# Reordering the opening of a two-layer hybrid decoder trunk on one Trainium2 core

## The chip, the cores and the metric

The kernel runs on one core of a Trainium2 chip. The metric is the device time of one execution in microseconds; the number to predict is the median over several runs. Engines are called PE (matrix products), DVE (vector), ACT (scalar), POOL and SP (which here only issues loads).

## What is computed

Each of two layers scales, shifts and projects its input, runs two attentions, and then a feed-forward part; scale and shift come from a condition vector `c`. The change touches only the beginning of the first layer:

```python
mod = jax.nn.silu(c) @ w_ada + b_ada                  # c: 1 x 1024, w_ada: 1024 x 6144
sh1, sc1, gt1, sh2, sc2, gt2 = jnp.split(mod, 6, axis=-1)
h = adaln(rms_norm(x, g_mix), sh1, sc1)               # x: 256 x 1024;  h * (1 + sc1) + sh1
proj = h @ w_in
q_a, k_a, v_a, q_b, k_b, v_b, gate_a, gate_b = jnp.split(proj, IN_OFFSETS, axis=-1)
```

All data is float32. `x` is 256 tokens (two tiles `t` of 128) by 1024 features (eight tiles `k` of 128).

## The kernel before

**Products in three parts.** An operand is split into a rounded high part and the rest, a low part. A product is three PE products: high by high, high by low, low by high. Before, the helper `mm3` (lines 505 to 507) issues the three one after the other. A block of weights of 512 KB ("half": two feature tiles of 512 columns) is loaded as float32 into `wraw`, rounded by ACT into the high part (line 423), and DVE subtracts it to give the low part (lines 429 and 918). `Stream` keeps three raw buffers of two halves and, in this stage, four slots `w0` to `w3` for split halves; a raw buffer takes its next load when both its halves are split, a slot when its products are done.

**The opening** (`lead`) computes `q_b`, `k_b` and `v_b` of the first layer, in four quarters of two feature tiles, since a quarter needs only the shift and scale of its 256 features. A quarter has three halves (one each for `q_b`, `k_b`, `v_b`), so 3 x 2 feature tiles x 2 token tiles x 3 parts = 36 products of 128x512. For its shift and scale a quarter needs `silu(c)` times eight 128x512 blocks of `w_ada`. These come as four "pieces" of two blocks (32 loads of 256 KB over all quarters). DVE sums them: `ada_quarter` (lines 313 and 315), one multiply-add `aq` per block, accumulated elementwise, 128 partitions in parallel. Then PE transposes the sum in four blocks (line 291), and DVE reduces along the row to a column (line 297), adds the bias and multiplies by the gain (lines 301 and 304), giving columns `sh` and `s1`. With those DVE makes `hf` (line 927), ACT the high part `hT_hi` (line 929), and DVE the low part `hT_lo` (line 933).

**Order.** The whole opening stands under a manual schedule: each engine executes in the order in which `lead` writes the code, and a waiting instruction holds all behind it on its engine. Which loads come in which order is written in `LOADS`, how many sum steps and weight splits lie between is in `AHEAD`, `LEAD0`, `READY`, `LEAD`. All loads go through SP's queue. The tables for the rotary embedding are made here too: `rope_sin` on ACT (lines 347 and 348, each with a load of a function table), `rope_tables` on DVE (line 366). After `lead` come `k_a` (128x256 products), `q_a`, the gates, and in between the steps of head norm, rotary embedding (lines 727 to 778) and attention (lines 793 to 857) for the heads.

Of the kernel before, what the change touches and what calls it, by code (L numbers as in the profile page):

```python
# [68 lines left out]
Q3 = 3  # L69
GAINS = 1  # L70
POW_LAG = 2

LOADS = "aaaarw4wawaaa"
AHEAD = (0, 2, 0)
LEAD0 = (0, 1, 0, 1, 5)
READY = (2, 0)
LEAD = (("h", "VhV", "v"), ("vh", "V", "v"), ("hVhV", "", "v"), ("hV", "", "vvvv"))
# [5 lines left out]
def kernel(ctx: ExitStack, tc: tile.TileContext, io):  # L85
# [42 lines left out]
    def load_x():  # L128
        nc.sync.dma_start(c8, io["c"][0].rearrange("(p k) -> p k", k=KT))
        nc.sync.dma_start(pos_i, io["positions"][0].rearrange("(t p) -> p t", p=P))  # L130
        nc.sync.dma_start(invf, io["cpack"][:, 0:HALF])
        for t in range(NT):
            nc.sync.dma_start(x_sb[:, t, :], io["x"][0, t * P:(t + 1) * P, :])
            if t == 0:
                nc.sync.dma_start(ident, io["cpack"][:, HALF:HALF + P])

    def load_rows():
        nc.sync.dma_start(grow[0:4 * KT, :], io["grow"])
        for l in range(DEPTH):
            o = (4 + 6 * l) * KT  # L140
            nc.sync.dma_start(grow[o:o + 6 * KT, :], io["b_ada"][l].rearrange("(r c) -> r c", c=P))
# [19 lines left out]

    def silu_c():
# [3 lines left out]
        nc.vector.tensor_scalar(out=cs, in0=cs, scalar1=0.5, scalar2=None, op0=ALU.mult)  # L166

# [139 lines left out]
    def ada_quarter(u):  # L307

        acc = ring(512, "aq")
        for k in range(KT):  # L310
# [15 lines left out]
    def rope_angles():  # L326
        nc.vector.tensor_copy(pos_f, pos_i)
        ang = work.tile([P, NT, HALF], F32, tag="rt", name="ang", bufs=3)
        for t in range(NT):
            nc.vector.tensor_scalar(out=ang[:, t, :], in0=invf, scalar1=pos_f[:, t:t + 1], scalar2=None, op0=ALU.mult)  # L330
        ns = [work.tile([P, NT, HALF], F32, tag="rt", name=nm("rtn"), bufs=3) for _ in range(2)]
# [532 lines left out]
    def lead():  # L864

        V = nc.vector
        stream.hold = True
        load_x()
        pieces = iter(range(16))

        def load_ada(n):
            for _ in range(n):
                ada_load(next(pieces))

        for o in LOADS:
            if o == "r":
                load_rows()
            elif o == "w":
                stream.load_next()
            elif o.isdigit():  # L880
                stream.between = lambda n=int(o): load_ada(n)
            else:
                load_ada(1)
        silu_c()
        rope_angles()
        stats = [ln_stats(t, (0, 1)) for t in range(NT)]
# [315 lines left out]
```

## Time and profile before

| | us |
|---|---|
| median of 3 runs (763.82 to 766.08) | 765.72 |
| the profiled execution: its time | 763.05 |
| its span, first to last instruction | 761.3 |
| PE busy | 723.2 (95%) |
| DVE busy | 600.1 (79%) |
| ACT busy | 431.3 (57%) |

A busy PE is not PE at its peak, because its instructions overlap and their ends are modelled; for products, the distance from one start to the next tells the cost. PEclk is the clock that was granted to PE, 1.00 being 2.4 GHz and 0.50 being 1.2 GHz.

### The profile page before, as it was taken

How to read it: one execution, taken by the hardware profiler on the slowest of the kernel's cores; microseconds unless marked ns; L12 is line 12 of the kernel's file. 1: busy time of each engine (PE TensorE's matmuls, PEld its weight loads, DVE VectorE, ACT ScalarE, POOL GpSimd, SP SyncE). 2: the span in 40 equal slices, each digit the busy share in tenths (PEclk: the TensorE clock that was granted, in tenths of full speed). 3: DMA queues.
4: the chain of work that ended last, by engine and by line, in shares of the span. 5: the costliest groups of instructions: out<-in, count | busy, mean ns of one | idle time of the engine just before them, and what ended most of it. 6: DMA issues, size and time to landing. Idle time of an engine off the chain costs nothing.

```text
span 761.3 us, 12132 instructions
## 1 busy us (share of the span) xinstructions
PE 723.2 (95%) x4601; PEld 638.2 (84%) x4601; DVE 600.1 (79%) x1107; ACT 431.3 (57%) x817; POOL 30.7 (4%) x23
## 2 busy tenths in 40 slices
PE   3879889999989999999998999999999999999997
PEld 2558678899869899899987888989988998999996
DVE  6978989989999988989889878987879755445532
ACT  6336369874457655554545457676546755555550
POOL 1003110000000000000000311000000000000000
PEclk9999999999999999999999999999999999999999
DMA  8968458867859999998893653663661856565511
GB/s 294 391 234 277 140 164 283 282 218 273 279 165 294 379 348 318 333 321 318 308 306 112 217 170 112 206 211 122 233 240 62 285 190 198 168 204 182 181 42 55
DMA packets 110538, 173.45 MB, mean 228 GB/s; under 512 B 4744, under 2 KB 68488, under 8 KB 110480
## 3 DMA queue, kind: packets, MB, share of 16 engines
q1 hardware_dynamic: 110480, 172.68, 66.8%
q8 instruction: 36, 0.59, 0.3%
q14 instruction: 22, 0.18, 0.1%
HBM read 171.62 MB, written 1.05 MB: 227 GB/s over the span
## 4 chain that ended last, share of the span: by engine, by line
PE 74%; DVE 11%; DMA 8%; ACT 2%; issue 2%; POOL 1%; SPq 0%; DVEq 0%; ACTq 0%; POOLq 0%
PE tmp L510 12%; PE tmp L512 11%; PE tmp L511 11%; PE acc L507 11%; PE acc L505 11%; PE acc L506 11%; DMA araw<-in_w_ada_dram 3%; DVE ada L262 2%; DVE w L429 2%; PE tmp L853 1%; POOL rs L734 1%; PE tmp L837 1%; PE acc L793 1%; DMA wraw<-in_w_out_dram 1%; DMA gt<-in_w_ada_dram 1%
## 5 line engine op out<-in xcount | busy, mean ns | idle before, releaser
L429 DVE TENSOR_TENSOR w<-wraw,w 128x1024 fp32r<-128x1024 f32 x144 | 174.4, 1220 | 51.5 <-ACT w L423 50.3
L423 ACT CAST w<-wraw 128x1024 fp32r<-128x1024 f32 x150 | 155.5, 1048 | 79.7 <-PE acc L507 46.4
L510 PE MATMUL tmp<-hT_hi,w 128*128 128x256 f32 x480 | 140.1, 292 | 1.1 <-DVE alo L857 1.1
L512 PE MATMUL tmp<-hT_hi,w 128*128 128x256 f32 x480 | 135.9, 283 | 0.0
L511 PE MATMUL tmp<-hT_lo,w 128*128 128x256 f32 x480 | 135.7, 283 | 0.0
L262 DVE SCALAR_TENSOR_TENSOR ada<-araw,cs,ada 128x512 f32<-128x512 f32 x140 | 104.3, 745 | 4.1 <-DMA araw<-in_w_ada_dram 2.9
L510 PEld LDWEIGHTS tmp<-hT_hi,w 128*128 128x128 f32 x480 | 91.5, 191 | 8.0 <-issue 4.4
L511 PEld LDWEIGHTS tmp<-hT_lo,w 128*128 128x128 f32 x480 | 91.7, 191 | 0.7
L512 PEld LDWEIGHTS tmp<-hT_hi,w 128*128 128x128 f32 x480 | 91.6, 191 | 0.3 <-issue 0.3
L505 PE MATMUL acc<-w,uhi 128*128 128x512 f32 x192 | 75.4, 393 | 0.0
L506 PE MATMUL acc<-w,uhi 128*128 128x512 f32 x192 | 74.9, 390 | 0.0
L507 PE MATMUL acc<-w,ulo 128*128 128x512 f32 x192 | 74.9, 390 | 0.0
L1093 ACT ACTIVATE relu<-tmp 128x256 f32<-128x256 f32 x56 | 21.5, 384 | 68.9 <-PE tmp L512 68.9
L507 PEld LDWEIGHTS acc<-w,ulo 128*128 128x128 f32 x192 | 36.1, 188 | 7.6
L505 PEld LDWEIGHTS acc<-w,uhi 128*128 128x128 f32 x192 | 36.1, 188 | 6.9
L506 PEld LDWEIGHTS acc<-w,uhi 128*128 128x128 f32 x192 | 36.1, 188 | 6.8
L505 PE MATMUL acc<-w,hT_hi 128*128 128x512 f32 x88 | 36.7, 419 | 2.6 <-ACT hT_hi L929 2.6
L507 PE MATMUL acc<-w,hT_lo 128*128 128x512 f32 x88 | 36.1, 410 | 2.8 <-DVE hT_lo L933 2.8
L506 PE MATMUL acc<-w,hT_hi 128*128 128x512 f32 x88 | 36.2, 411 | 1.2 <-DVE w L429 0.7
L423 ACT CAST kv<-wraw 128x1024 fp32r<-128x1024 f32 x21 | 22.1, 1053 | 24.6 <-PE acc L507 19.8
L429 DVE TENSOR_TENSOR ahi<-wraw,ahi 128x1024 fp32r<-128x1024 f32 x18 | 22.0, 1221 | 15.0 <-ACT ahi L423 14.9
L429 DVE TENSOR_TENSOR kv<-wraw,kv 128x1024 fp32r<-128x1024 f32 x21 | 25.6, 1221 | 9.6 <-ACT kv L423 9.5
(221 smaller groups left out, 1726.2 us busy)
## 6 DMA issues: line engine op xcount, KB each, us to landing
araw<-in_w_ada_dram SPq DMA_DIRECT2D x80, 512.0 KB, 6.6
wraw<-in_w_up_dram SPq DMA_DIRECT2D x32, 1024.0 KB, 5.6
wraw<-in_w_down_dram SPq DMA_DIRECT2D x32, 1024.0 KB, 5.0
wraw<-in_w_in_dram SPq DMA_DIRECT2D x28, 1024.0 KB, 6.1
wraw<-in_w_out_dram SPq DMA_DIRECT2D x8, 1024.0 KB, 4.9
wraw<-in_w_in_dram SPq DMA_DIRECT2D x12, 512.0 KB, 6.6
wraw<-in_w_o_swa_dram SPq DMA_DIRECT2D x8, 512.0 KB, 3.6
wraw<-in_w_o_moba_dram SPq DMA_DIRECT2D x8, 512.0 KB, 5.3
```

The source lines that it names most:

```text
L262: nc.vector.scalar_tensor_tensor(out=acc, in0=raw[:, k, :], scalar=cs[:, kk:kk + 1], in1=(bz if kk == 0 else acc), op0=ALU.mult, op1=ALU.add)
L423: nc.scalar.copy(hi, r)
L429: ins = nc.vector.tensor_tensor(out=lo, in0=r, in1=hi.bitcast(F32), op=ALU.subtract)
L505: nc.tensor.matmul(ps, lhsT=lh, rhs=rh, start=start, stop=False)
L506: nc.tensor.matmul(ps, lhsT=lh, rhs=rl, start=False, stop=False)
L507: nc.tensor.matmul(ps, lhsT=ll, rhs=rh, start=False, stop=stop)
L510: nc.tensor.matmul(ps, lhsT=wh, rhs=ah, start=start, stop=False)
L511: nc.tensor.matmul(ps, lhsT=wh, rhs=al, start=False, stop=False)
L512: nc.tensor.matmul(ps, lhsT=wl, rhs=ah, start=False, stop=stop)
L734: nc.gpsimd.tensor_tensor(out=rs, in0=ss, in1=mhalf[:, :NT * nh].rearrange("p (t h) -> p t h", h=nh), op=ALU.pow)
L793: nc.tensor.matmul(pss[i][:, os], lhsT=qT[hp, pair, qs], rhs=kT[hp, kp, ks], start=True, stop=True)
L1093: nc.scalar.activation(r, ps, AF.Relu)
```

## The change

- The sums of quarters 1 and 2 move from DVE to PE. `pe_sums` multiplies each block by a 128x32 operand `cz` whose first column is `silu(c)` and whose others are zero: eight float32 products of 32x512. The eight write four groups of 32 PSUM partitions, two products to a group. ACT copies the result (`arow`), and four products by a column of ones (`columns`) sum over partitions and turn the row into columns. Quarters 0 and 3 stay on DVE (`dve_sums`), but use `columns` too, so the transposes and the reduction of line 297 are gone.
- Loads come quarter by quarter: four pieces of `w_ada`, then the three halves of that quarter. Positions, frequencies, the identity matrix, gain and bias rows go through ACT's queue instead of SP's.
- Within a quarter PE does high by high for all three halves first, then low by high and high by low, half after half.
- `x` is normalised and transposed half by half, the second halves' copies on DVE. PE multiplies ones by ones before (24 products of 128x128) and between (8).
- `rope_sin` moves to quarter 0, the rotary tables ahead of quarter 2.

```diff
+WAKE = (24, 8)
+EARLY = 3
...
     def load_x():
         nc.sync.dma_start(c8, io["c"][0].rearrange("(p k) -> p k", k=KT))
-        nc.sync.dma_start(pos_i, io["positions"][0].rearrange("(t p) -> p t", p=P))
-        nc.sync.dma_start(invf, io["cpack"][:, 0:HALF])
         for t in range(NT):
             nc.sync.dma_start(x_sb[:, t, :], io["x"][0, t * P:(t + 1) * P, :])
-            if t == 0:
-                nc.sync.dma_start(ident, io["cpack"][:, HALF:HALF + P])
+        nc.scalar.dma_start(pos_i, io["positions"][0].rearrange("(t p) -> p t", p=P))
+        nc.scalar.dma_start(invf, io["cpack"][:, 0:HALF])
+        nc.scalar.dma_start(ident, io["cpack"][:, HALF:HALF + P])
...
+    def pe_sums(u):
+        ps = tmp_t()
+        for kk in range(KT):
+            i = kk % 4
+            nc.tensor.matmul(ps[32 * i:32 * i + 32, :], lhsT=cz[:, kk, :], rhs=ada_raw[4 * u + kk // 2][:, kk % 2, :],
+                             start=(kk < 4), stop=(kk >= 4), skip_group_check=True)
+        rows = ring(512, "arow")
+        nc.scalar.copy(rows, ps)
+        return rows
+
+    def columns(rows):
+        ps = tmp_t()
+        for i in range(4):
+            nc.tensor.matmul(ps[:, i:i + 1], lhsT=rows[:, i * P:(i + 1) * P], rhs=ones[:, 0:1], start=True, stop=True,
+                             skip_group_check=True)
+        return ps
...
     def lead():
...
+        load_x()
+        load_ada()
+        stream.load_next()
+        stream.between = load_ada
+        stream.load_next()
+        stream.load_next()
+        load_ada()
+        load_gains()
+        silu_c()
+        load_rows()
+        rope_angles()
...
+        wake(WAKE[0])
...
+        def part(ps, q, left, w, first=False, last=False):
+            for k in range(2):
+                for t in range(NT):
+                    T.matmul(ps[t], lhsT=left[:, 2 * q + k, t * P:(t + 1) * P], rhs=w[:, k, :],
+                             start=(first and k == 0), stop=(last and k == 1))
+        cast()
+        cast()
+        apply(0, cols)
+        cast()
+        rope_sin()
+        for _ in range(3):
+            low()
         for q in range(4):
...
+            halves = [stream.get() for _ in range(3)]
+            stream.between = load_ada if q == 0 else None
+
+            def rest(i):
+                part(groups[i], q, hT_lo, halves[i][1])
+                part(groups[i], q, hT_hi, halves[i][2], last=(q == 3))
+                stream.release(halves[i][0])
+
+            for i in range(3):
+                part(groups[i], q, hT_hi, halves[i][1], first=(q == 0))
+            cast()
+            low()
+            rest(0)
+            if q == 3:
+                rest(1)
+                rest(2)
+                break
+            rest(1)
+            if q < 2:
+                acc = pe_sums(q + 1)
+            part(groups[2], q, hT_lo, halves[2][1])
+            cols = columns(acc)
+            part(groups[2], q, hT_hi, halves[2][2])
+            cast()
+            if q == 1:
+                tabs = rope_tables(0)
+                nc.vector.tensor_scalar(out=nsink, in0=nsink, scalar1=-1.0, scalar2=None, op0=ALU.mult)
+                sum_steps(3, EARLY)
+            apply(q + 1, cols)
+            stream.release(halves[2][0])
+            cast()
+            if q == 1:
+                low()
+                sum_steps(3, 3)
+                acc = sum_steps(3, 5 - EARLY)
+                low()
+            else:
+                low()
+                low()
+            if q == 0:
+                rope_gains()
+                load_rest()
```

`cast` is ACT's rounding of the next half, `low` DVE's subtraction, `apply` lines 301, 304 and then `hT_hi`, `hf`, `hT_lo`. Lines of the changed kernel in the rows below are its own: 984 is `part`, 325 `pe_sums`, 335 `columns`, 440 `cast`, 961 `low`, 970 to 975 `apply`, 383 the rotary tables, 328 the copy to `arow`.

The order on PE in quarter 0. Before, where `w0` to `w2` are the halves of `q_b`, `k_b`, `v_b`:

```order
L505 MATMUL acc_1_276<-w0_1_244,hT_hi_105 128x512
L506 MATMUL acc_1_276<-w0_1_244,hT_hi_105 128x512
L507 MATMUL acc_1_276<-w0_1_244,hT_lo_106 128x512
L505 MATMUL acc_2_277<-w0_1_244,hT_hi_105 128x512
L506 MATMUL acc_2_277<-w0_1_244,hT_hi_105 128x512
L507 MATMUL acc_2_277<-w0_1_244,hT_lo_106 128x512
...
L291 MATMUL tmp_9_315<-cpack_81,aq_2_306 128x128 x4
L505 MATMUL tmp_7_280<-w2_1_264,hT_hi_105 128x512
L506 MATMUL tmp_7_280<-w2_1_264,hT_hi_105 128x512
L507 MATMUL tmp_7_280<-w2_1_264,hT_lo_106 128x512
```

And now:

```order
L984 MATMUL acc_1_282<-w0_1_288,hT_hi_107 128x512
L984 MATMUL acc_2_283<-w0_1_288,hT_hi_107 128x512
...
L984 MATMUL acc_1_282<-w0_1_288,hT_lo_108 128x512
L984 MATMUL acc_2_283<-w0_1_288,hT_lo_108 128x512
...
L325 MATMUL tmp_10_357<-ahi_1_126,cz_94 32x512 x2
L325 MATMUL tmp_10_357<-alo_1_136,cz_94 32x512 x4
L325 MATMUL tmp_10_357<-qT_1_141,cz_94 32x512 x2
L984 MATMUL tmp_8_286<-w2_1_304,hT_lo_108 128x512
L984 MATMUL tmp_9_287<-w2_1_304,hT_lo_108 128x512
...
L335 MATMUL tmp_11_372<-ones_87,arow_1_366 128x1 x4
L984 MATMUL tmp_8_286<-w2_1_304,hT_hi_107 128x512
```

The three parts of a product stood side by side and now stand apart (high by high, line by line, ahead of the first `hT_lo`), and eight products `cz` stand ahead of the last part of the third half, with the copy on ACT and `columns` behind them.

The order on DVE ahead of quarter 2's columns. Before:

```order
L315 SCALAR_TENSOR_TENSOR aq_3_331<-kv_1_151,cs_93,aq_3_331 128x512 x4
L315 SCALAR_TENSOR_TENSOR aq_3_331<-gt_1_156,cs_93,aq_3_331 128x512 x2
L918 TENSOR_TENSOR w2_2_401<-wraw_4_259,w2_2_401 128x1024
L918 TENSOR_TENSOR w3_2_404<-wraw_4_259,w3_2_404 128x1024
L297 TENSOR_REDUCE cols_3_409<-tmp_10_396 128x4
L301 TENSOR_TENSOR sh_0_0_99<-cols_3_409,gcol_94 128x2
L301 TENSOR_TENSOR s1_0_0_95<-cols_3_409,gcol_94 128x2
L304 SCALAR_TENSOR_TENSOR s1_0_0_95<-s1_0_0_95,gcol_94 128x2
L927 TENSOR_SCALAR hf_3_414<-ln_1_185,s1_0_0_95,sh_0_0_99 128x256 x2
L933 TENSOR_TENSOR hT_lo_106<-hf_3_414,hT_hi_105 128x512
```

And now:

```order
L961 TENSOR_TENSOR w2_2_416<-wraw_4_292,w2_2_416 128x1024
L383 TENSOR_TENSOR ct_1_463<-gqk_84,sincos_106 128x4x32
...
L1022 TENSOR_SCALAR nsink_86<-nsink_86 128x16
L313 TENSOR_SCALAR aq_2_474<-gt_2_327,cs_93 128x512
L315 SCALAR_TENSOR_TENSOR aq_2_474<-gt_2_327,cs_93,aq_2_474 128x512
L315 SCALAR_TENSOR_TENSOR aq_2_474<-araw_4_330,cs_93,aq_2_474 128x512
L301 TENSOR_TENSOR sh_0_0_101<-tmp_13_450,gcol_96 128x2
L301 TENSOR_TENSOR s1_0_0_97<-tmp_13_450,gcol_96 128x2
L304 SCALAR_TENSOR_TENSOR s1_0_0_97<-s1_0_0_97,gcol_96 128x2
L972 TENSOR_SCALAR hf_3_481<-ln_1_215,s1_0_0_97,sh_0_0_101 128x256 x2
L975 TENSOR_TENSOR hT_lo_108<-hf_3_481,hT_hi_107 128x512
L961 TENSOR_TENSOR w3_2_459<-wraw_4_292,w3_2_459 128x1024
```

The sums of quarter 2 (`aq_3`) are gone from it, and the rotary tables and three steps of quarter 3's sum (`aq_2`) stand ahead of quarter 2's columns `sh` and `s1`.

The order on ACT, around the loads of its function tables. Before, at quarter 2:

```order
L423 CAST w3_2_404<-wraw_4_259 128x1024
L929 ACTIVATE hT_hi_105<-ln_1_185,sh_0_0_99,s1_0_0_95 128x256 x2
L347 ACT_TABLE_LOAD
L347 ACTIVATE sincos_104<-sincos_104 128x128
L348 ACT_TABLE_LOAD
L348 ACTIVATE pos_f_103<-pos_f_103 128x2
L423 CAST w0_3_422<-wraw_5_323 128x1024
L423 CAST w1_3_477<-wraw_5_323 128x1024
L929 ACTIVATE hT_hi_105<-ln_1_185,sh_0_0_99,s1_0_0_95 128x256 x2
```

And now, from quarter 0 on:

```order
L440 CAST w0_1_288<-wraw_1_129 128x1024
L440 CAST w1_1_290<-wraw_1_129 128x1024
L970 ACTIVATE hT_hi_107<-ln_1_215,sh_0_0_101,s1_0_0_97 128x256 x2
L440 CAST w2_1_304<-wraw_2_132 128x1024
L364 ACT_TABLE_LOAD
L364 ACTIVATE sincos_106<-sincos_106 128x128
L365 ACT_TABLE_LOAD
L365 ACTIVATE pos_f_105<-pos_f_105 128x2
L440 CAST w3_1_323<-wraw_2_132 128x1024
L328 COPY arow_1_366<-tmp_10_357 128x512
L440 CAST w0_2_381<-wraw_3_145 128x1024
L970 ACTIVATE hT_hi_107<-ln_1_215,sh_0_0_101,s1_0_0_97 128x256 x2
```

The two loads of tables stood behind `hT_hi` of quarter 2 and now stand behind the third rounding of quarter 0, ahead of the fourth.

## Rows read from the trace of the kernel before

**Rows 1.** Profile page, busy time: engine, busy us, share, instructions.

```profile
PE 723.2 (95%) x4601; PEld 638.2 (84%) x4601; DVE 600.1 (79%) x1107; ACT 431.3 (57%) x817; POOL 30.7 (4%) x23
```

**Rows 2.** Windows of the opening: from:to, length, busy time by engine, PEclk, DMA share, GB/s.

```profile
18.46:32.30 13.84, 11.92 (x40) 8.41 (x40) 13.20 (x21) 4.58 (x6) 0.00 (x0) 1.00 1.08 390
50.90:56.20 5.30, 0.01 (x1) 0.04 (x1) 5.09 (x8) 0.00 (x0) 0.00 (x0) 0.99 0.00 0
56.20:69.60 13.40, 13.38 (x54) 10.90 (x55) 12.70 (x27) 8.74 (x12) 0.00 (x0) 0.88 0.67 229
```

**Rows 3.** Timeline of PE in the opening: start, length, line, operation, [idle before].

```profile
18.46 0.79 PE L505 MATMUL acc<-w,hT_hi 128*128 128x512 f32 x1 [2.01 <-ACT hT_hi L929]
...
22.34 0.63 PE L505 MATMUL acc<-w,hT_hi 128*128 128x512 f32 x1
22.76 0.63 PE L506 MATMUL acc<-w,hT_hi 128*128 128x512 f32 x1
...
50.27 0.39 PE L506 MATMUL acc<-w,hT_hi 128*128 128x512 f32 x1
50.49 0.39 PE L507 MATMUL acc<-w,hT_lo 128*128 128x512 f32 x1
56.19 1.09 PE L291 MATMUL tmp<-cpack,aq 128*128 128x128 f32 x4 [5.31 <-DVE aq L315]
...
69.33 0.39 PE L507 MATMUL tmp<-w,hT_lo 128*128 128x512 f32 x1
```

**Rows 4.** Groups of lines on DVE, 0 to 69.6 us: busy, mean ns, idle before.

```profile
L429 DVE TENSOR_TENSOR w<-wraw,w 128x1024 fp32r<-128x1024 f32 x9 | 10.7, 1217 | 3.4 <-ACT w L423 3.4
L315 DVE SCALAR_TENSOR_TENSOR aq<-araw,cs,aq 128x512 f32<-128x512 f32 x11 | 8.3, 752 | 0.4
...
L366 DVE TENSOR_TENSOR ct<-gqk,sincos 128x128 f32<-128x128 f32 x4 | 1.1, 288 | 0.0
```

**Rows 5.** Timeline of SP's queue: the first load of x.

```profile
2.16 0.43 SPq L133 DMA_DIRECT2D x_sb<-in_x_dram  x1
```

**Rows 6.** Timeline of DVE in the opening.

```profile
17.28 0.16 DVE L301 TENSOR_TENSOR sh<-cols,gcol 128x2 f32<-128x2 f32 x1
...
58.04 0.16 DVE L301 TENSOR_TENSOR sh<-cols,gcol 128x2 f32<-128x2 f32 x1
...
59.63 0.69 DVE L933 TENSOR_TENSOR hT_lo<-hf,hT_hi 128x512 fp32r<-128x512 f32 x1 [0.39 <-ACT hT_hi L929]
...
67.47 1.27 DVE L731 TENSOR_REDUCE ss<-sq 128x8 f32<-128x512 f32 x2
```

**Rows 7.** A window in quarter 1, columns as in rows 2.

```profile
35.40:39.00 3.60, 3.60 (x11) 2.77 (x10) 3.46 (x6) 0.37 (x1) 0.00 (x0) 0.53 1.09 388
```

**Rows 8.** Chain of waits, 0 to 140 us: start, length, link.

```profile
32.94 6.66 DMA araw<-in_w_ada_dram
...
116.34 0.80 PE tmp L853 x8
...
119.35 0.22 PE tmp L837 x2
```

**Rows 9.** Timeline of PE around a narrow product.

```profile
116.06 0.28 PE L512 MATMUL tmp<-hT_hi,w 128*128 128x256 f32 x1
116.27 0.87 PE L853 MATMUL tmp<-pT,kv 128*64 128x256 f32 x8
```

**Rows 10.** DMA issues by destination, 0 to 110 us: count, KB each, us to landing.

```profile
wraw<-in_w_in_dram SPq DMA_DIRECT2D x12, 512.0 KB, 6.6
araw<-in_w_ada_dram SPq DMA_DIRECT2D x12, 256.0 KB, 5.6
```

**Rows 11.** Timeline of ACT in the opening.

```profile
38.63 1.05 ACT L423 CAST w<-wraw 128x1024 fp32r<-128x1024 f32 x1 [3.24 <-PE acc L507]
...
44.83 1.28 ACT L347 ACT_TABLE_LOAD   x1
```

**Rows 12.** A window behind the opening, columns as in rows 2.

```profile
76.00:140.00 64.00, 57.88 (x418) 49.08 (x417) 58.59 (x145) 43.13 (x110) 5.78 (x2) 1.00 0.63 206
```

More of the change, by code (lines that the diff above doesn't have):

```diff
@@ L864, in lead, with load_ada @@
     def lead():
-        V = nc.vector
+        V, A, T = nc.vector, nc.scalar, nc.tensor
         stream.hold = True
+        pieces = iter(range(16))
+        def load_ada():
+            for _ in range(4):
+                ada_load(next(pieces))
         load_x()
-        pieces = iter(range(16))
-        def load_ada(n):
-            for _ in range(n):
[L873 to L883, printed above, removed]
@@ new lines, in rows_turn @@
+        def rows_turn(t, h, copy):
+            ps = ln_transpose(t, h)
+            copy(xnT[:, 4 * h:4 * h + 4, t * P:(t + 1) * P], ps.rearrange("p (j s) -> p j s", s=P))
+        rows_scale(0)
+        for t in range(NT):
+            rows_turn(t, 0, A.copy)
+        gps = tmp_t()
+        T.transpose(gps[:, :P], grow, ident)
+        A.activation(gcol[:, :4 * KT], gps[:, :4 * KT], AF.Copy, scale=float(D) ** 0.5)
+        A.copy(gcol[:, 4 * KT:], gps[:, 4 * KT:P])
+        wake(WAKE[1])
+        rows_scale(1)
@@ L923, in ready_apply, with cast, low, apply @@
+        acc = sum_steps(0, 6)
+        for t in range(NT):
+            rows_turn(t, 1, V.tensor_copy)
+        cols = columns(acc)
+        def cast():
+            stream.split_next("later")
+        def low():
+            lo, raw, hi = stream.later.pop(0)
+            V.tensor_tensor(out=lo, in0=raw, in1=hi.bitcast(F32), op=ALU.subtract)
+        def apply(q, cols):
+            ada_affine(0, 0, q, cols, 2, (0, 1))
             x = xnT[:, 2 * q:2 * q + 2, :]
@@ L931, in ready_apply @@
+                V.tensor_scalar(out=hf[:, i, :], in0=x[:, i, :], scalar1=s1[0][0][:, j:j + 1],
+                                scalar2=sh[0][0][:, j:j + 1], op0=ALU.mult, op1=ALU.add)
             js = slice(2 * q, 2 * q + 2)
[L932 to L955 removed]
@@ L957, in lead @@
-        tabs = []
-        ready(0)
+            V.tensor_tensor(out=hT_lo[:, js, :], in0=hf, in1=hT_hi[:, js, :].bitcast(F32), op=ALU.subtract)
         groups = [[acc_t() for _ in range(NT)] for _ in range(2)]
         groups.append([tmp_t() for _ in range(NT)])
-        for q in range(4):
-            for i, g in enumerate(groups):
-                go = (lambda: ready(q + 1)) if i == READY[0] and q < 3 else None
-                if go and READY[1] == 0:
-                    go()
-                proj_half(g, stream.get(), 512, 2 * q, go if READY[1] else None)
+        def part(ps, q, left, w, first=False, last=False):
+            for k in range(2):
+                for t in range(NT):
+                    T.matmul(ps[t], lhsT=left[:, 2 * q + k, t * P:(t + 1) * P], rhs=w[:, k, :],
+                             start=(first and k == 0), stop=(last and k == 1))
```

111 lines of the change are left out of this document (36 added, 75 removed).

## The prediction

> **What bounds the kernel now.** I read the page first: PE is busy for 723.2 of 761.3 us [rows 1], so time is to be won only where PE is not dense. Then the windows by stage: the opening, up to 69.6 us, is such a place, and behind it PE is nearly full. In the opening the loads run at 390 GB/s while DVE is busy for 13.2 of 13.8 us; later the loads stand still for 5.3 us in which DVE alone works and PE does nothing [rows 2]. Third, PE's timeline: its first product starts at 18.46 us and the last of the opening, the 144th, at 69.33. Dense, two starts lie 0.228 us apart, so 144 products would need 32.8 us; the opening takes 51.1. A gap of 5.31 ends on `aq`, the sum for quarter 3 [rows 3]. DVE is the cause: a step of a sum costs 0.75 us and its issue (0.78 from start to start), 32 of them 25; a low part of weights costs 1.22 at most, fourteen of them 16 [rows 4]. DVE bounds the opening; loads come second.
>
> **The change, part by part.** I lay the new order on the span's clock, with durations of the profiled run (763.05 us; its span is 761.3, and the median of the runs, 765.72, is 2.7 above).
>
> *Start.* `x` is issued at 2.16 us now, behind four loads of 0.43 [rows 5], three of which go to ACT, as small as they are; loads come 1.0 earlier. This gains little, since ACT must now round two halves ahead of the first `hT_hi`. By the pace of the loads (39.6 us for 15 pieces and 8 halves of 0.52 MB each, see quarter 2 below) the second of these lands behind 4 pieces and 2 halves: 17 fewer, 8.9 MB or 22.9 us less, and 1.0 earlier, at 15.7. Two roundings of 0.95 from start to start and the first half of `hT_hi` (0.5) put the first product at 18.0. Were the halves earlier, 17.0 (`x` earlier); if ACT were late by one rounding, 19.0. The 24 products of ones run while PE has nothing else.
>
> *Quarter 0.* 36 products of 0.228 are 8.2 us. Before, products started 0.43 apart at first (22.34, 22.76 [rows 3]). PEclk's column says 1.00 there, but a later stretch with the same distance has 0.53 [rows 7]: this is the 1.2 GHz level. The ten slow products cost 2.0 us; the products of ones may prevent that (0) or not (2.0); I take 1.3, since about 2 us stay idle ahead of the first product.
>
> *Sums on PE.* No row shows a product of 32x512. A float32 product stands as two records: the eight records of L853 are four products in the code. A record of 128 columns costs 0.11 (0.22 for two [rows 8]), so I price one of 512 at 0.44, and 16 one after the other at 7.0: the upper end. L853 has four records of 256 and four of 128, 1.32 by that price, but lasts 0.80 [rows 8]: with two column groups it runs 1.65 times as fast. The change has four groups; if all ran at once, 16 records would take 1.8: the lower end. By 1.65 they take 4.3. Between 1.8 and 4.3 I take 3.0. `columns` I price at 0.5, as the four transposes it replaces. The copy to `arow` (some 0.6) hides behind four products (0.9) of the third half; without them it would be on the path. From `sh` to the first product it takes 1.2 (17.28 [rows 6] to 18.46), of which the last four products cover 0.9: 0.3 stays.
>
> By the Trainium skill, page "TensorE: Matmul & The Clock Gate", Part 3 (packing small matmuls), products in different column groups run at the same time and a pack takes hardly longer than one product. The row agrees in kind (1.65 for two groups; none shows four). By that rule a sum would be at the lower end, quarter 2 would wait for DVE instead (below), and the forecast would be 757.0 in place of 757.3.
>
> PE must also change between wide and narrow products twice per sum: ahead of L853 the start lies 0.21 behind the one before, where 256 columns otherwise take 0.12 (both in [rows 9]). This 0.1 is within the 3.0.
>
> *Quarter 1* starts at 18.0 + 8.2 + 1.3 + 3.0 + 0.5 + 0.3 = 31.3, and *quarter 2*, by PE, at 31.3 + 8.2 + 3.0 + 0.5 + 0.3 = 43.3. DVE must be there in time. Its queue has the low part of the half `w2_2_416` first, which needs a load. Of the loads (256 and 512 KB [rows 10]), before, 15 pieces and 8 halves had landed at 39.6 (32.94 + 6.66 [rows 8]). This half needs 12 pieces, 8 halves and 0.26 MB of gains: 1.3 MB or 3.4 us less, and 1.0 earlier: 35.2. Then 1.0 on ACT (as 1.05 [rows 11]), 1.2 for the low part, 2.3 for the tables (8 of 0.288 [rows 4]), and 2.1 for three steps of quarter 3's sum, ahead of `sh`: free at 41.8. `columns` of quarter 2 is done at 42.1, so PE decides, by 0.3. If DVE were late, PE would wait: this is the tightest place.
>
> *Quarter 3.* DVE, from 42.1: 2.3 up to `hT_lo` (58.04 to 60.3 [rows 6]), a low part, five steps, two low parts: 3 x 1.15 + 5 x 0.78 = 7.4, so `sh` at 51.8 and the first product at 53.0; PE would be ready at 52.0. The half needed last has landed at 46. The end is 53.0 + 8.2 = 61.2, against 69.56 (69.33 + 0.23): 8.4 us.
>
> *Other moves.* The two table loads on ACT (1.28 each [rows 11], 3.1 in all with the two short operations) come at about 19.4 to 22.5, when ACT would wait for the fourth half, due at 23.7; were that half earlier, they would delay it. One low part (1.2) moves behind the opening, off PE's path as long as its half is needed later. The queue of SP now has gains and then halves of quarter 2, which wait for a raw buffer; the buffer is free at 21.4 (two low parts behind `hT_lo` of quarter 0), and the load isn't due before 27.
>
> *Behind the opening* the same instructions follow in nearly the same order, on all engines. DVE reaches the head norms at 67.47 now [rows 6]; in the new order it has done three of the four low parts by 58 and waits only for the first group's products, which end at about 57.5 (20 products after 53.0): 9 to 10 us earlier. So both shift alike, and the sum stands: **8.4 us** less, 754.7 by the profiled run, **757.3** against the median.
>
> **The rivals.**
> - *More is won*: the clock stays up, sums take 1.8 us, and of the 6.1 us that PE idles from 76 to 140 [rows 12] a part goes, since one chain on DVE starts earlier. The first two bring quarter 1 forward by 2.5, but quarter 2 by 0.3 only, since DVE then decides; with 3 us of the third, 754.0. Against it: DVE is busy for 58.6 of these 64 us.
> - *Part is given back*: the last group closes later against the end than before, so the norms, the powers on POOL and the attentions lag PE, which waits in 76 to 140. In quarter 3 the first group closes 3.6 us ahead of the end (16 products), before it was 5.5 (24). If PE waits for that difference of 1.9 at two of its stations there, 761.1. For it: a full DVE; against it: DVE reaches the norms 9 us earlier itself.
> - *Sums don't run side by side*: 7.0 us each at full clock, 4.0 more than I take, twice: 757.3 + 8.0 = 765.3, no change. So the change would not do what it is built on. Against it: L853.
> - *Slower*: the same at 1.2 GHz, since a narrow stretch may not keep the clock: 14.0 each, 22.0 more: 779.3. It decides from 7.2 us a sum on (3.0 + 8.4 / 2). For it: from 35.4 to 39 the clock was down although PE was busy throughout [rows 7]; against it: dense products stand right ahead of each sum.
>
> **How the numbers follow.** Forecast 0.60, own range 755.5 to 761 (0.3 less with quick sums; 1.3 more for each slow one, 0.7 for the clock, and some 0.4 for DVE; and 1.5 less by which the profiled run and the median may differ); more 0.12; part back 0.13; side by side fails 0.07; slower 0.08. The range 752.0 to 763.0 takes in the first three and leaves out 0.15 of the rest, and a little at both ends. A measurement of this kernel can tell about 0.3%, 2.3 us: below 763.4 is faster. The first three cases lie there, save 0.02 of the third: faster 0.83; within, 0.02 and the 0.07: 0.09; slower 0.08.
>
> **What would show it.** L325's 16 records in 2 to 4 us; no `aq` wait of 5 us on PE; the first `k_a` products at about 61 in place of 69.6, and `ss` on DVE at 58. Wrong would be: L325 over 7 us; PE waiting for `sh` ahead of quarter 2 for over 2 us (then the tables stand in the wrong place); or a `k_a` at 61 with PE idle for more than 8 us in the 64 us that follow 67 (then it was given back).

## The result, and the profile after

The changed kernel takes **757.92 us**, the median of 4 runs (755.65 to 758.79), beside 764.77 for the kernel before in the same runs (762.71 to 766.08). The ratio is 0.9895, with a 95% interval of [0.9863, 0.9926]: faster by 0.7 to 1.4%. The two medians lie 6.9 us apart; their quotient, 0.9910, is inside that interval. Run again beside other kernels, the same program took 756.23 against 763.76, again 0.9895 [0.9849, 0.9941]. The profiled run took 755.65 us with a span of 753.9, 7.4 less than the 761.3 before. It is the fastest of its four: its mean granted clock is 1.000, the others have 0.990 to 0.997.

The page, busy time (beside [rows 1]):

```profile
PE 730.7 (97%) x4713; PEld 645.3 (86%) x4713; DVE 587.2 (78%) x1090; ACT 431.2 (57%) x817; POOL 32.0 (4%) x24
```

PE is busy for 7.5 us more (it has the products of ones and the sums besides), DVE for 12.9 less, and the span is shorter.

Windows of the opening, a quarter each, and the 64 us behind it (columns as in [rows 2]):

```profile
18.29:29.90 11.61, 11.50 (x61) 7.84 (x61) 6.37 (x10) 7.69 (x11) 0.00 (x0) 1.00 1.08 390
29.90:42.56 12.66, 11.52 (x60) 7.83 (x61) 9.73 (x25) 4.62 (x7) 0.00 (x0) 1.00 1.08 392
42.56:52.07 9.51, 9.41 (x45) 7.50 (x45) 8.89 (x15) 4.14 (x6) 0.00 (x0) 1.00 0.80 288
52.07:60.41 8.34, 8.34 (x37) 6.79 (x37) 6.95 (x9) 5.98 (x9) 0.00 (x0) 1.00 0.90 306
68.30:132.30 64.00, 57.75 (x422) 49.20 (x421) 58.26 (x145) 43.09 (x110) 5.78 (x2) 1.00 0.65 212
```

Before, the opening held 5.3 us in which PE did nothing and a stretch at 0.53 of the clock [rows 2, 7]. Now PE is busy for 40.8 of 42.1 us, and PEclk is 1.00 throughout. Behind the opening PE idles 6.25 us of 64, much as before (6.12 [rows 12]).

Timeline of PE in the opening (start, length, line, operation, count, [idle before]):

```profile
15.25 1.02 PE L335 MATMUL tmp<-ones,aq 128*128 128x1 f32 x8
18.29 2.15 PE L984 MATMUL acc<-w,hT_hi 128*128 128x512 f32 x8 [2.02 <-ACT hT_hi L970]
...
24.90 0.62 PE L325 MATMUL tmp<-ahi,cz 128*32 128x512 f32 x2
...
26.22 0.60 PE L325 MATMUL tmp<-qT,cz 128*32 128x512 f32 x2
26.75 1.21 PE L984 MATMUL tmp<-w,hT_lo 128*128 128x512 f32 x4
27.80 0.95 PE L335 MATMUL tmp<-ones,arow 128*128 128x1 f32 x8
28.61 1.17 PE L984 MATMUL tmp<-w,hT_hi 128*128 128x512 f32 x4
29.90 2.15 PE L984 MATMUL acc<-w,hT_hi 128*128 128x512 f32 x8
...
42.56 2.14 PE L984 MATMUL acc<-w,hT_hi 128*128 128x512 f32 x8 [1.14 <-ACT hT_hi L970]
...
60.41 0.28 PE L522 MATMUL tmp<-w,hT_hi 128*128 128x256 f32 x1
```

Against [rows 3]: the first eight products take 2.15 us; before, two starts lay 0.43 apart at that place. A sum, with its 16 records, lasts from 24.90 to 26.75, 1.85 us. The wait of 5.31 for `aq` is gone; one of 1.14 ahead of quarter 2 is left. The opening ends at 60.41 in place of 69.56.

Timeline of DVE around that wait and at the end (beside [rows 6]):

```profile
36.65 1.23 DVE L961 TENSOR_TENSOR w<-wraw,w 128x1024 fp32r<-128x1024 f32 x1 [1.49 <-ACT w L440]
37.79 0.28 DVE L383 TENSOR_TENSOR ct<-gqk,sincos 128x128 f32<-128x128 f32 x1
...
39.49 0.48 DVE L313 TENSOR_SCALAR aq<-gt,cs 128x512 f32<-128x512 f32 x1
...
41.46 0.15 DVE L301 TENSOR_TENSOR sh<-tmp,gcol 128x2 f32<-128x2 f32 x1
...
57.38 0.69 DVE L748 TENSOR_REDUCE ss<-sq 128x8 f32<-128x512 f32 x1 [0.74 <-ACT sq L744]
```

`columns` of quarter 2 stand on PE from 39.43 to about 40.2, but `sh` follows at 41.46 only: a low part that waits for its half, eight table products and three steps of quarter 3's sum stand ahead of it. DVE decides there.

### The profile page after: what moved, and what is told of

Same layout as the page of the kernel before. It is cut to its first block, busy times and chain, and to the rows that moved or that the text cites. A ratio compares the mean times of both kernels' runs of the same rounds, so it can differ in the third digit from the quotient of the medians.

```text
span 753.9 us, 12320 instructions
## 1 busy us (share of the span) xinstructions
PE 730.7 (97%) x4713; PEld 645.3 (86%) x4713; DVE 587.2 (78%) x1090; ACT 431.2 (57%) x817; POOL 32.0 (4%) x24
## 3 DMA queue, kind: packets, MB, share of 16 engines
HBM read 171.62 MB, written 1.05 MB: 229 GB/s over the span
## 4 chain that ended last, share of the span: by engine, by line
PE 72%; DVE 13%; DMA 7%; ACT 3%; issue 2%; POOL 2%; SPq 0%; ACTq 0%; DVEq 0%; POOLq 0%
PE tmp L527 11%; PE acc L524 11%; PE acc L522 11%; PE acc L523 11%; PE tmp L528 10%; PE tmp L529 10%; DMA araw<-in_w_ada_dram 4%; DVE ada L259 2%; DVE w L446 2%; PE acc L984 2%; POOL rs L751 1%; ACT w L440 1%; PE tmp L870 1%; DMA wraw<-in_w_up_dram 1%; PE acc L810 1%
## 5 line engine op out<-in xcount | busy, mean ns | idle before, releaser
L446 DVE TENSOR_TENSOR w<-wraw,w 128x1024 fp32r<-128x1024 f32 x137 | 166.3, 1221 | 48.1 <-ACT w L440 46.8
L446 DVE TENSOR_TENSOR qT<-wraw,qT 128x1024 fp32r<-128x1024 f32 x21 | 25.6, 1220 | 8.3 <-ACT qT L440 8.3
L527 PE MATMUL tmp<-hT_hi,alo 128*128 128x256 f32 x112 | 31.8, 284 | 0.0
L528 PE MATMUL tmp<-hT_lo,alo 128*128 128x256 f32 x112 | 31.7, 283 | 0.0
```

The costliest lines, as they stand in the source:

```text
L446: ins = nc.vector.tensor_tensor(out=lo, in0=r, in1=hi.bitcast(F32), op=ALU.subtract)
L527: nc.tensor.matmul(ps, lhsT=wh, rhs=ah, start=start, stop=False)
L528: nc.tensor.matmul(ps, lhsT=wh, rhs=al, start=False, stop=False)
```

## The experiments

The first four take one part of the change away, or keep one part alone.

**The sums back on DVE.**

```diff
-        sums = {0: dve_sums(0), 3: dve_sums(3)}
+        sums = {q: dve_sums(q) for q in range(4)}
...
+            if q < 2:
+                acc = sum_steps(q + 1, 8)
             cast()
             low()
...
-            if q < 2:
-                acc = pe_sums(q + 1)
```

> Everything of the change stays, but the sums of quarters 1 and 2 are on DVE again, placed where DVE has time (ahead of the low part that waits for the quarter's fourth half). Theory (the relief of DVE is what carries the gain): 16 steps of 0.77 us come back, 12.3 us. 3.8 us of the first eight fit where DVE now waits for a load; so quarter 1 starts about 2 us later, quarter 2 about 6 us later than its 42.56, and quarter 3 about 6 later than its 52.07. The opening (up to the first k_a product, 60.41 now) ends at 66 to 67, and the time is 5 to 6.5 us above the change's. Rival (the new order of products and loads carries the gain, DVE has room for the sums): opening within 2 us of 60.4, time within 2 us of the change's.

Measured: 765.53 us (10 runs), a ratio to before of 0.9994 [0.9964, 1.0023]; the opening ends at 68.92. The whole gain is gone. PE's timeline of this run:

```profile
30.27 1.02 PE L335 MATMUL tmp<-ones,aq 128*128 128x1 f32 x8 [1.48 <-DVE aq L315]
42.80 1.02 PE L335 MATMUL tmp<-ones,aq 128*128 128x1 f32 x8 [2.77 <-DVE aq L315]
48.47 3.78 PE L984 MATMUL acc<-w,hT_hi 128*128 128x512 f32 x8 [2.89 <-ACT hT_hi L970]
```

PE waits 4.2 us for sums and 2.9 for `hT_hi` ahead of quarter 2, and behind the last of these idle stretches eight products take 3.78 us in place of 2.15. PEclk is 0.50 there, the lower level of the clock (a window, columns as in [rows 2]):

```profile
48.47:52.05 3.58, 3.58 (x8) 2.81 (x9) 3.16 (x5) 2.33 (x3) 0.00 (x0) 0.50 0.02 5
```

That, and a first product at 19.65, go with a loss (7.6 us by the medians) above the 5 to 6.5 expected; the mean granted clock of the ten runs is 0.985, that of the change's first four 0.995. With the sums on DVE in this place the reordered rest gives no gain. So the gain needs the relief of DVE: it ends waits of PE, and with them slow products behind the waits. Other places for the sums on DVE were not tried.

**All products of a sum in one column group.**

```diff
-            i = kk % 4
-            nc.tensor.matmul(ps[32 * i:32 * i + 32, :], lhsT=cz[:, kk, :], ...
-                             start=(kk < 4), stop=(kk >= 4), ...
+            nc.tensor.matmul(ps[0:32, :], lhsT=cz[:, kk, :], ...
+                             start=(kk == 0), stop=(kk == KT - 1), ...
```

(The copy to `arow` and `columns` take the 32 rows that are left.)

> The eight products of a sum on PE all go into the first column group, one after the other, in place of four groups. Theory (the four groups run at once, four rounds of 0.46 us): 16 records one after the other take 7.2 us in place of 1.85, so quarter 1 starts 5.3 us later, quarter 2 about 9.5 later (10.7 of sums, less the 1.14 that PE waits for DVE there now). The opening ends near 70 and the time is 8 to 9.5 us above the change's, as slow as before. Rival (a sum is short because its products have only 32 rows of output, whatever the group): still about 2 us a sum, time within 1 us of the change's.

Measured: 766.24 us (10 runs), 1.0009 [0.9987, 1.0031]. The profile is of the slowest of the ten (769.3): quarter 0 begins at 20.14, since the clock was down ahead of it, and the opening ends at 73.42, later than expected. The first sum in this run:

```profile
28.34 1.90 PE L324 MATMUL tmp<-ahi,cz 128*32 128x512 f32 x4
30.08 3.60 PE L324 MATMUL tmp<-alo,cz 128*32 128x512 f32 x8
33.52 1.88 PE L324 MATMUL tmp<-qT,cz 128*32 128x512 f32 x4
```

16 records from 28.34 to 35.40: 7.06 us, 0.44 a record, where four groups take 1.85. So the four groups run at once, and without that the change is worth nothing. The records keep 0.44 to the end, and PEclk is 1.00 from 28.34 to 35.40, so these 7 us of narrow products do not lose the clock; the rival that had it slower than before falls with that.

**Without the products of ones.**

```diff
-WAKE = (24, 8)
+WAKE = (0, 0)
```

> The 32 products of ones ahead of the first product are left out. Theory (they are what holds the clock at 2.4 GHz for quarter 0): the first ten or so products start 0.43 us apart again, as before the change; quarter 1 starts 2.0 later (near 31.9), of which 1.1 is hidden where PE waits for DVE ahead of quarter 2; the opening ends 0.9 later, near 61.3, and the time is 0.5 to 1 us more. Rival (the transposes and the dense order of the products would hold the clock without them): products 0.23 apart from 18.3 on, no difference.

Measured: 761.31 us (6 runs), 0.9929 [0.9906, 0.9953]; the opening ends at 63.58. PE's timeline:

```profile
14.95 1.97 PE L559 MATMUL tmp<-cpack,ln 128*128 128x128 f32 x8 [1.31 <-ACT ln L933]
16.71 1.71 PE L335 MATMUL tmp<-ones,aq 128*128 128x1 f32 x8
19.69 3.78 PE L982 MATMUL acc<-w,hT_hi 128*128 128x512 f32 x8 [1.27 <-ACT hT_hi L968]
```

The first eight products take the 3.78 us that stood beside a PEclk of 0.50 above. By their times, nearly double, the clock is at its lower level not only in quarter 0 but for the transposes (1.97 for eight records, after the change 1.06) and `columns` ahead of it (1.71, after the change 1.02), and these lie on the path to `sh`. So the first product comes 1.4 us later, the first sum 4.2 (29.07 against 24.90) and the end 3.2. The kind of effect is the theory's; its size at the end of the opening is over three times what I had written, and the time is 3.4 us above the change's by the medians where I had 0.5 to 1. So about a third of the gain hangs on the products of ones (0.7% without them, 1.05% with them, by the ratios, whose intervals overlap).

**The sums on PE alone, in the kernel before.**

```diff
-        units = [ada_quarter(q) for q in range(4)]
+        units = [ada_quarter(0), pe_quarter(1), pe_quarter(2), ada_quarter(3)]
```

(`pe_quarter` yields eight times without work, then issues the products of `pe_sums`, the copy, `columns`, and the bias and gain. `cz` is made as in the change, and the angles of the rotary embedding take other buffers, as there.)

> The kernel before with one part of the change alone: the sums of quarters 1 and 2 on PE, in the place where their transposes stood; loads, order of the products, products of ones and all else as before. Theory (this part pays only together with the reordered rest): the sum for quarter 3 still starts behind a low part whose cast comes at 47.9 on ACT, behind the table loads, so that PE waits for it as before; ahead of quarters 1 and 2 PE now waits for the copy to arow and the columns, some 3 us each. The opening ends at 69 to 71 (before 69.56), the time is within 2 us of before's. Rival (DVE's work as a sum bounds the opening, 12.3 us less of it is enough): opening at 61 to 63, time 6 to 8 us below before's.

Measured: 768.95 us (10 runs), 1.0036 [1.0011, 1.0061]: not faster, rather slower. The opening ends at 77.14, later than I had expected; 13 `k_a` products (1.6 us) lie ahead of that end, before the change one, and the profile is of the slowest of the ten runs (771.11). Timelines of PE and DVE:

```profile
31.78 1.05 PE L325 MATMUL tmp<-ones,arow 128*128 128x1 f32 x8 [0.78 <-ACT arow L322]
...
60.87 1.08 PE L294 MATMUL tmp<-cpack,aq 128*128 128x128 f32 x4 [5.31 <-DVE aq L338]
```

```profile
32.70 1.23 DVE L452 TENSOR_TENSOR w<-wraw,w 128x1024 fp32r<-128x1024 f32 x1 [10.59 <-ACT w L446]
...
45.67 2.36 DVE L941 TENSOR_TENSOR w<-wraw,w 128x1024 fp32r<-128x1024 f32 x2 [7.77 <-ACT w L446]
...
53.59 1.23 DVE L452 TENSOR_TENSOR w<-wraw,w 128x1024 fp32r<-128x1024 f32 x1 [3.38 <-ACT w L446]
54.73 0.48 DVE L336 TENSOR_SCALAR aq<-gt,cs 128x512 f32<-128x512 f32 x1
```

The time that DVE is spared turns into idle time of DVE (10.59 and 7.77 us), because its queue goes on behind casts that ACT has put behind the copy. The sum for quarter 3 still begins late, and PE waits the same 5.31 us for it as before. Neither the sums on PE (in this place) nor the new order pays alone; together they give 1%.

**The same kernel again.** In two of the profiles so far (sums on DVE, one column group) the clock was down ahead of quarter 0 although nothing is edited there, so the changed kernel ran once more as it is.

> The changed kernel once more, as it is. Its four times so far rise as the mean granted clock falls (755.65 us at 1.000 to 758.79 at 0.992), and two of the experiments, alike up to 13 us, ran their second block of products of ones and the transposes at half speed and started quarter 0 at 19.7 and 20.1 in place of 18.29. Theory (the products of ones do not hold the clock in every execution, and the profile shown is a lucky one): times between 755.5 and 761, a median of 758 to 759, and where a profile shows a drop of PEclk ahead of 20 us, quarter 0 starts 1.4 to 1.9 later. Rival (the drops came with the edits): times within 1 us of 757.9, quarter 0 at 18.3.

Measured: 756.23 us (753.77 to 757.8), quarter 0 at 17.51, the opening's end at 59.92, the clock up. The median expected, 758 to 759, did not come, nor did the times keep within 1 us of 757.9: they spread over 4 us, as the first four did over 3.1. Whether the clock holds in every execution this profile cannot say; the table further down collects what all of them show.

**Three products of a half side by side again.**

```diff
             for i in range(3):
                 part(groups[i], q, hT_hi, halves[i][1], first=(q == 0))
+                if i < 2:
+                    rest(i)
             cast()
             low()
-            rest(0)
```

(and without the two `rest(1)` that follow)

> In the changed kernel the three products of a half stand side by side again (high by high, low by high, high by low) for the first two halves of each quarter, all else as it is. Theory (the order matters little once DVE has time for the low parts): quarter 0 waits 0.2 for hT_lo and 0.2 for a low part, the others 0.2 each for hT_lo, some 1 us in all, of which a part is hidden where PE waits for DVE ahead of quarter 2: the time is 0.5 to 1 us above the change's. Rival (high by high first is what keeps PE dense): each quarter waits 1.2 us for hT_lo or a low part, as quarters 0 and 1 did before the change, and the time is 3 to 5 us more.

Measured: 755.51 us (754.69 to 756.09), 0.9888 [0.9849, 0.9927]; the opening ends at 61.00, 1.1 later than that of the kernel as changed in the same job, and the time is the same. High by high first is worth about 1 us of the opening and nothing that can be measured at the end.

**`hT_hi` ahead of the second cast, tables later.**

```diff
         cast()
-        cast()
         apply(0, cols)
         cast()
+        cast()
...
             if q == 3:
+                tabs = rope_tables(0)
+                nc.vector.tensor_scalar(out=nsink, in0=nsink, scalar1=-1.0, ...
                 rest(1)
```

(and without the two lines ahead of quarter 2)

> Two moves in the changed kernel: hT_hi of quarter 0 ahead of the second cast on ACT, and the rope tables and nsink on DVE behind the third low part of quarter 3 in place of ahead of quarter 2. Theory: the first product no longer waits for the second cast and starts at 17.4 in place of 18.3; PE no longer waits 1.1 for DVE ahead of quarter 2; the opening ends 2 us earlier, near 58.4, and the time falls by 1 to 2 us. Rival (the tables are then late for the head norms, or quarter 1 waits for a load): the opening ends earlier, but the time is the change's within 0.7.

Measured: 757.84 us, the median of 8 runs with one of 1837.3 us in it; without that one it is 757.09, and the ratio, which leaves it out, is 0.9913 [0.9884, 0.9941]. The profile, of the slowest of the other seven (759.92), can't judge the edit, because the clock fell ahead of quarter 0, where the edit changes nothing yet. PE's timeline tells it:

```profile
13.49 3.62 PE L908 MATMUL tmp<-ones 128*128 128x128 f32 x16
...
20.40 3.51 PE L984 MATMUL acc<-w,hT_hi 128*128 128x512 f32 x8 [1.27 <-ACT hT_hi L970]
```

The second row of ones takes 3.62 us (1.95 in the changed kernel), the transposes behind it are late, and so is `sh`. Quarter 0 begins at 20.40, 2.1 later than in the change. The two moves were taken up again below, with the clock held.

**More products of ones.**

```diff
-WAKE = (24, 8)
+WAKE = (30, 4, 8, 7)
```

(4 between the first two groups of transposes, 7 behind `columns` of quarter 0)

> More products of ones in the changed kernel: 30 in place of 24 at first, 4 between the first two transposes, 8 as now, and 7 behind the columns of quarter 0, where PE has nothing to do for 2 us. Theory (the idle stretches ahead of quarter 0 are where the clock falls in some executions): PEclk stays at 1.00 up to 30 us, quarter 0 starts at 18.3 to 18.6 and its products lie 0.23 apart, and the times lie closer together, with a median 1 to 2.5 us below the changed kernel's own in this job. Rival (the drops do not come from idle stretches): the same scatter and median as the changed kernel's, or 0.5 more for the products in the way.

Measured: 756.09 us (754.36 to 757.39), 0.9889 [0.984, 0.9939]. The profile is as the theory has it, the time is not lower. Over all profiles the clock ahead of quarter 0 stands like this:

| run | PE idle ahead of the first, second transposes | PEclk, 10 to 18 us | quarter 0 begins |
|---|---|---|---|
| after | 0.60, 1.27 | 1.00 | 18.29 |
| after_again | 0.56, 1.31 | 1.00 | 17.51 |
| side | 0.45, 1.63 | 1.00 | 17.68 |
| dve_sums | 0.86, 1.86 | 0.79 | 19.65 |
| serial | 1.98, 1.35 | 0.57 | 20.14 |
| hi_tables | 2.16, 1.50 | 0.57 | 20.40 |
| wake_more | 0.17, 0.28 | 1.00 | 18.01 |

With 24 and 8 products the clock was held in three profiles and lost in three, although these kernels are alike up to 13 us. It was lost in those with the longest idle stretch ahead of the transposes. The length alone does not decide: the changed kernel (first row) idles 2.02 us a little later, ahead of quarter 0, and its products there keep 2.15 us for eight. The four kernels below have the longer row of ones too, and all of them have PEclk at 1.00 here. That the clock holds with more products of ones is what all five profiles show; that it pays is not shown: the medians of the kernel as changed and of this one, run together, lie within 0.2 us.

The last four were run together, all with more products of ones.

**`hT_hi` ahead of the second cast:**

```diff
-WAKE = (30, 4, 8, 7)
+WAKE = (30, 4, 8, 3)
...
         cast()
-        cast()
         apply(0, cols)
         cast()
+        cast()
```

> The run with more products of ones, with 3 in place of 7 behind the columns of quarter 0, and with hT_hi of quarter 0 ahead of the second cast on ACT. Theory (quarter 2 is set by DVE, which waits for a load, whatever PE does): quarter 0 starts at 17.1 to 17.4 in place of 18.0 and quarter 1 near 28.8 in place of 29.6, but quarter 2 at 42.2 as in that run; the opening ends at 60.0 and the time is that run's within 0.7 us (a ratio to before of 0.987 to 0.991). Rival (PE is the bound all along): all of the 0.8 us reaches the end of the opening (59.2) and the time.

Measured: 755.79 us (6 runs), 0.9891 [0.9863, 0.9919]; quarter 0 at 17.89, quarter 2 at 42.35, the opening's end at 60.23. Quarter 0 did not come to the 17.1 to 17.4 expected, since `hT_hi` now waits 0.55 us for DVE's `sh` and `s1`. The time is that of the run before it, as the theory had it.

**The tables later as well:**

```diff
             if q == 1:
-                tabs = rope_tables(0)
-                nc.vector.tensor_scalar(out=nsink, in0=nsink, scalar1=-1.0, ...
...
             if q == 3:
+                tabs = rope_tables(0)
+                nc.vector.tensor_scalar(out=nsink, in0=nsink, scalar1=-1.0, ...
```

> The same with the rope tables and nsink behind the third low part of quarter 3 as well. Theory (with the tables gone DVE is ahead of quarter 2 and PE sets the opening, but the 2 us of tables then stand ahead of the head norms): quarter 2 at 40.3 without a wait, quarter 3 near 49.8, the opening ends at 58.1, 1.9 earlier than with more products of ones alone; on DVE the first head norm comes 0.5 to 1 us later than before this edit, so of the 1.9 about half is left at 110 us, and the time is 0.5 to 1.5 us lower (a ratio to before of 0.986 to 0.990). Rival (DVE has time for the tables there): 1.9 us lower all the way.

Measured: 758.01 us (6 runs), 0.9918 [0.9887, 0.995]; the opening ends at 62.26, 2.2 later than with more products of ones alone, instead of 1.9 earlier. DVE's timeline ahead of quarter 2, and PE's there:

```profile
39.27 0.48 DVE L313 TENSOR_SCALAR aq<-gt,cs 128x512 f32<-128x512 f32 x1 [0.88 <-DMA gt<-in_w_ada_dram]
40.03 0.75 DVE L315 SCALAR_TENSOR_TENSOR aq<-gt,cs,aq 128x512 f32<-128x512 f32 x1 [0.28 <-DMA gt<-in_w_ada_dram]
41.09 0.75 DVE L315 SCALAR_TENSOR_TENSOR aq<-araw,cs,aq 128x512 f32<-128x512 f32 x1 [0.30 <-DMA araw<-in_w_ada_dram]
41.76 0.15 DVE L301 TENSOR_TENSOR sh<-tmp,gcol 128x2 f32<-128x2 f32 x1
```

```profile
42.86 3.66 PE L987 MATMUL acc<-w,hT_hi 128*128 128x512 f32 x8 [1.38 <-ACT hT_hi L973]
```

My theory was wrong: the tables filled time in which DVE would else wait for the pieces of quarter 3. Without them `sh` comes no earlier (41.76, with them 41.25 in the run before), and this time the clock fell behind PE's idle stretch (3.66 for eight products, PEclk 0.52). What sets quarter 2 is the loads, by way of the three early steps: the next run has the tables there but not the steps, and no wait is left.

**The sum of quarter 3 on PE too:**

```diff
-        sums = {0: dve_sums(0), 3: dve_sums(3)}
+        sums = {0: dve_sums(0)}
...
-            if q < 2:
-                acc = pe_sums(q + 1)
+            acc = pe_sums(q + 1)
```

(and without the eight steps)

> More products of ones (30, 4, 8, 7), and the sum of quarter 3 on PE too, like those of quarters 1 and 2. Theory (PE is what the end of the opening waits for once DVE is in time): no wait ahead of quarter 2, which starts 1.0 earlier, near 41.1; the sum's 1.85 us then stand on PE's path, quarter 3 starts near 52.6 in place of 51.7 and the opening ends 0.9 later, near 60.9; the time is 0 to 1 us more than with more products of ones alone (ratio to before 0.988 to 0.993). Rival (6 us less of DVE work ahead of the head norms pay behind the opening): the time 1 to 3 us less.

Measured: 758.87 us (6 runs), 0.9928 [0.9903, 0.9953]: 3.1 us above the two runs beside it that differ from it least (`hT_hi` ahead, small loads), by the medians. No wait ahead of quarters 1 to 3 is left:

```profile
30.46 2.15 PE L987 MATMUL acc<-w,hT_hi 128*128 128x512 f32 x8
...
42.09 2.14 PE L987 MATMUL acc<-w,hT_hi 128*128 128x512 f32 x8
...
53.72 2.15 PE L987 MATMUL acc<-w,hT_hi 128*128 128x512 f32 x8
```

Each quarter takes 11.63 us, so PE alone sets the opening, which ends at 62.06. With two sums on PE and quarter 3's on DVE it ends at 60.02 (more products of ones). Two of three is a better split than none or all (one of three was not tried), and DVE's further relief buys nothing behind the opening.

**The small loads back on SP:**

```diff
+        nc.sync.dma_start(pos_i, ...)
+        nc.sync.dma_start(invf, io["cpack"][:, 0:HALF])
         for t in range(NT):
             nc.sync.dma_start(x_sb[:, t, :], io["x"][0, t * P:(t + 1) * P, :])
-        nc.scalar.dma_start(pos_i, ...)
-        nc.scalar.dma_start(invf, io["cpack"][:, 0:HALF])
-        nc.scalar.dma_start(ident, io["cpack"][:, HALF:HALF + P])
+            if t == 0:
+                nc.sync.dma_start(ident, io["cpack"][:, HALF:HALF + P])
```

> More products of ones (30, 4, 8, 7), and the three small loads pos, invf and ident back on the queue of SP, two of them ahead of x. Theory (every later load comes by their issue later, and quarter 2 waits for one): x and all behind it 0.9 to 1.3 later, quarter 0 near 19.0, quarter 2 near 43.2, the opening ends 1 us later, near 61, and the time is 0.7 to 1.3 us more than with more products of ones alone (ratio to before 0.989 to 0.993). Rival (the 16 engines' bytes set the loads, and the issue of three small ones costs nothing): no difference, opening at 60.0.

Measured: 755.74 us (6 runs), 0.9883 [0.9856, 0.991]; quarter 0 at 18.69, quarter 2 at 42.61, the opening's end at 60.46. 0.4 us of the opening and nothing in the time: moving these loads is no part of the gain. No version ran measurably faster than the change. Three parts of it were not taken away by themselves: the order of the loads, `x` half by half, and `rope_sin` in quarter 0.

## Why the prediction was right, and where it was off

The forecast, 757.3 us, is 0.6 below the measured median, and its mechanism holds in the main: two sums fewer on DVE end the wait for `aq`, and nothing of size takes its place. But DVE's work was not all of that wait. Ahead of it, in the kernel before, DVE itself stood idle for 3.37 us, behind a rounding that ACT had put behind its two table loads (the first at 44.83 [rows 11]):

```profile
47.85 1.99 ACT L423 CAST w<-wraw 128x1024 fp32r<-128x1024 f32 x2
48.91 1.22 DVE L429 TENSOR_TENSOR w<-wraw,w 128x1024 fp32r<-128x1024 f32 x1 [3.37 <-ACT w L423]
```

The text put the gap of 5.31 down to DVE's work alone. What it gains to move `rope_sin` by itself in the kernel before was not tried; with the sums back on DVE the move is in place, and nothing is gained.

That the number came so close is in part luck. The forecast took 8.4 us off 765.72; the medians of the result lie 6.9 apart, but the kernel before has 764.77 there, 0.95 lower, with a fourth run. The end of the opening moved by 9.15 us where the sum had 8.4. By its steps:

- *Start*: 18.0, was 18.29 and 17.51. The wait is for `hT_hi` behind the second rounding, as said, but the sum had it by two errors that cancel: the second half of weights landed at about 16.6 and not at 15.7, and one rounding, not two, stood behind it. That the small loads gain little is shown. ACT ahead of quarter 0:

```profile
15.41 1.04 ACT L440 CAST w<-wraw 128x1024 fp32r<-128x1024 f32 x1 [0.75 <-DMA wraw<-in_w_in_dram]
16.69 1.04 ACT L440 CAST w<-wraw 128x1024 fp32r<-128x1024 f32 x1 [0.24 <-DMA wraw<-in_w_in_dram]
17.64 1.09 ACT L970 ACTIVATE hT_hi<-ln,sh,s 128x256 fp32r<-128x256 f32 x2
```

- *Clock in quarter 0*: I took 1.3 us of loss, since PE would idle some 2 us ahead of it; it did idle 2.02, and the loss was 0 in the profile. The price of having no products of ones, 2.0, was too low: the term left out the transposes and `columns`, which the lower level slows too. It cost 4.2 up to the first sum and 3.2 at the end.
- *Sums*: 3.0 taken, 1.85 measured, at the lower end (1.8). The row of L853, with two groups, was too weak a guide for four. The Trainium skill's rule (page "TensorE: Matmul & The Clock Gate", Part 3), that a pack in different column groups takes hardly longer than one product, fits better: 16 records take what four take one after the other, and quarter 2 waits for DVE, as it would by that rule. With one group, 7.06 against the 7.0 of the upper end. The text reads 0.12 for a product of 256 columns in [rows 9], which don't show it; the `k_a` products of the kernel before do (69.55, 69.67).
- *`columns`*: 0.5 taken, 0.8 measured (27.80 to 28.61).
- *Quarter 1*: 31.3 predicted, 29.90 measured: the clock's 1.3 and the sum's 1.15 less, against some 0.3 more for the start and for `columns` each, and 0.45 more in the wide products (6.61 for the first 28 in place of 6.38, 1.05 for the four behind the sum in place of 0.91) and the step to quarter 1 (0.1).
- *Quarter 2*: 43.3 against 42.56. "PE decides, by 0.3" failed: `columns` was done at 40.24 in place of 42.1, DVE was free at 41.46 in place of 41.8, so DVE decided, by 1.2, and PE waited 1.14. DVE's 41.8 had errors that nearly cancel: the low part came 0.4 later, the tables took 1.7 in place of 2.3. The text named this as the tightest place and said that quicker sums would bring quarter 2 forward by 0.3 only; it was 0.7. I took the tables for part of the limit; the last experiments show that the loads of quarter 3's pieces stand behind them.
- *Quarter 3 and end*: 53.0 and 61.2, measured 52.07 and 60.41. The wait of 1.0 for DVE that the text has ahead of quarter 3 did not come.
- *Behind the opening*: "the sum stands" is nearly so. DVE's first row sums of the attention (their reciprocal) moved by 8.9 us (111.36 to 102.47), the first residual by 8.1 (208.86 to 200.74), the last by 7.4. Two executions of the changed kernel differ by as much on their way: the second is 0.5 ahead of the first at 102 us, 1.5 at 130, 0.4 at 201 and 1.9 at the end. So whether the 1.75 us are given back by the change or lost to that scatter stays open. The rival that had them given back between 76 and 140 us is not seen: PE is busy for 57.75 of 64 us there, before 57.88.

So an early gain of 0.75 and a late loss of 1.75 leave 7.4 us in the profiles, 1.0 short of the sum. That the median came out within 0.6 of the forecast is the scatter of the runs and the lower start, not a finer agreement.

## What to carry to other kernels

Work moved off a full engine is won only if what stands behind it in that engine's queue, and in the queues that feed it, can move up too; the same two sums gave nothing in the old order, and the new order gave nothing without them. When two engines share such a job, look for the split at which both are just in time, and ask for each wait that is left what would be late next: here, behind DVE's tables, the loads. Idle time just ahead of dense products can cost twice, since work at the lower level of the clock may follow it.

## What was unexpected of the hardware

- Programs that are alike up to 13 us got different clocks there: in three profiles, with idle stretches of PE of up to 1.63 us ahead of the transposes, the granted clock stayed at 1.00, in three, with 1.86 to 2.16, it fell to 0.50 for some microseconds. The length alone does not tell: the clock stayed behind an idle stretch of 2.02 us ahead of quarter 0 (the change) and one of 1.44 ahead of quarter 2 (its second run), and fell behind one of 1.38 ahead of quarter 2 (tables later).
- The column PEclk can say 1.00 while products run at the lower level: without products of ones it does so from 18 to 30 us, although eight products take 3.78 us, as they do beside a PEclk of 0.50 with the sums back on DVE.
- The same 24 products of ones, issued at 0.99 us each time, took from 7.01 to 8.44 us. Where they ended soonest (7.01 with one column group, 7.06 with `hT_hi` and the tables moved) PE then idled longest (1.98 and 2.16 us) and the clock fell; but it fell behind 8.16 too (sums on DVE) and stayed behind 8.13 (second run of the change).
